# Modulation by selector products, gate weights converted early, and ScalarE's copies of the turned maxima ahead of its exponential

## The chip, the cores and the metric

The kernel runs on one core of a Trainium2 chip. The time is device microseconds of one execution of the whole program. The core has five engines, each with its own queue of instructions in order: TensorE (PE; its weight loads are shown apart as PEld), VectorE (DVE), ScalarE (ACT), GpSimd (POOL) and SyncE (SP, which here issues the transfers between the chip's memory and the core). They meet through semaphores. TensorE writes its sums to PSUM banks, from which VectorE and ScalarE read.

## The reference, cut to what matters

A backbone of two layers over 2,048 latent tokens (a grid of 32 rows of 64) and 256 context tokens, each of width 1,024. Per layer:

```
shift, scale, gate = split(silu(c) @ w_ada + b_ada, 3)      # 3 x 1024; context tokens have their own c
h   = rmsnorm(x) * (1 + scale) + shift
z   = h @ w_in                                              # one projection, cut into 12 column groups
A   = Re(fft2(u)) @ w_four            * silu(gate A)        # 4 Fourier groups of 64
B   = softmax(q k + bias | q kc) [v; vc] * silu(gate B)     # 6 heads of 64, window 8 x 16, plus context keys
C   = norm(gla(q, k, v, decay))       * silu(gate C)        # 4 heads, linear attention in both directions
x   = x + gate * (concat(A, B, C) @ w_out)
```

At the end stands a last RMSNorm. Context tokens pass through the first layer with the same weights and read only context tokens.

## The kernel before

**Order.** The order of nearly all work is written by hand. `Pin` (L64) wraps an engine so that each call keeps the place it has in the program; every instruction recorded that way bears the line of that wrapper, L72, so the profile's groups are told apart by the names of their tiles. PSUM has four names of banks, `a`, `b`, `c`, `pj`, with two buffers each.

**Modulation in the prologue** (L1683 to L1774). The rows of `w_ada` for shift and scale come in eight chunks of 1 MB and 256 columns (`load_r`, L168). `mm_r` multiplies a chunk by the two columns `sil` (the token's and the context's silu(c)): the 8 blocks of the contraction go to 4 groups of TensorE's columns, so the bank holds four partial sums of two rows, on partitions 0, 32, 64 and 96. `fin_r` (L180) copies the first sum with ScalarE, adds the other three with VectorE, and turns the 2x256 row into columns by two transposes into the same bank; VectorE adds the bias (`ada_sc`). `mod` (L189) makes from it the factor `modA` and the summand `modS`, with a common scale for float16. To find the largest value over all partitions it makes a diagonal `dg` with ScalarE, multiplies it by `ones` and reduces the product.

**Weights.** `w_steps` (L468) turns a group of columns of `w_in` into a high and a low float16 part, as a list of small steps: the load, four maxima over quarters (VectorE), empty steps (`lag`), the product with `dg`, the inverse, four high parts (ScalarE) and four low ones (VectorE). `fx` and `fg` are the Fourier group's input and gate.

**Norm and first projections.** Token tiles go in pairs. `norm_a` squares and sums (ScalarE), `norm_b` multiplies (VectorE), `put_a` transposes (TensorE, banks b and c), `put_e` scales by modulation (`hu`) in four groups of two blocks, and writes the high part `hx` (a cast on VectorE) and the low part (a difference on GpSimd, in the last group on VectorE). `four_x` and `four_g` (L320, L327) project. Pair 0 is the context (block 4); the steps of `fg` hang on `put_e`, two after each group:

```
norm_a(1)
norm_b(1)
put_e(s0, 0, [pairs[0], pairs[0] + 1], ra[0], V=v, S=s, G=g, hook=lambda k: step(wg, 2))
```

**Attention** (`na`, from L519). The work is cut into units (p, b): a pair of heads p and a block b of 512 latent tokens (256 context tokens for b = 4); 15 units in layer 0, 12 in layer 1. `fill` (L889) merges the steps of a unit by due times between 0 and 1: packs of scores (TensorE into bank a, VectorE adds the bias table into `pt`), `flush` (the pack's exponential: ScalarE `pt`, its float16 part `ph`, GpSimd the rest `pl`), the products with the values (bank c), the next unit's q and its largest scores, and side jobs. The largest scores of a row (`mh`) are turned by TensorE into bank b and copied into `Q2s` (step `fin`, L729), of which the next unit's scores are made: one copy on ScalarE, one on VectorE. A unit's result is finished in the next one by four steps of `tail` (L757): the last multiplies the gate `gt` by the reciprocal sum, the output `ob` by that, both on GpSimd, and stores `mixd`. Their due times are 0, 1, 2 and 3 parts of a unit.

**Side jobs.** During the attention of layer 0 the modulation of layer 1 is made in steps (`chunk`, L136): load, matmuls, four additions on VectorE onto a row that holds the bias, one empty step, two transposes and a VectorE copy. Chunks 8 to 11 are the gate of the residual and are stored. `wo_scale` (L1481) finds the scale of the output weights, with two empty steps ahead of its product with `dg`.

Of the kernel before, what the change touches and what calls it, by code (L numbers as in the profile page):

```python
# [9 lines left out]
F32 = mybir.dt.float32  # L10
# [67 lines left out]
def body(ctx: ExitStack, tc: tile.TileContext, a, out, dbg=None):  # L78
# [52 lines left out]
    def ada(l, pool):  # L131
        nw = pool.tile([P, KB], F32, tag="ada_nw", name="ada_nw", bufs=1)
        sc = pool.tile([P, 2, 16], F32, tag="ada_sc", name="ada_sc", bufs=1)
        nc.sync.dma_start(out=nw, in_=a["nwcol"][l])

        def chunk(c, pool=pool):  # L136
# [4 lines left out]
            def s0():  # L141
                d["w"] = pool.tile([P, KB * 256], F32, tag="ws", name="ws", bufs=1).rearrange("p (k n) -> p k n", k=KB)
                nc.sync.dma_start(out=d["w"], in_=a["w_ada"][l, c])
                d["row"] = pool.tile([P, 256], F32, tag="row", name="ada_row", bufs=1)[0:2, :]
                nc.sync.dma_start(out=d["row"], in_=a["b_ada"][l:l + 1, c * 256:(c + 1) * 256].to_broadcast([2, 256]))

            def s1():
                pt = d["pt"] = bank("b")
                for k in range(KB):
                    o = k % 4 * 32  # L150
                    te.matmul(out=pt[o:o + 2, 0:256], lhsT=sil[:, k, :], rhs=d["w"][:, k, :], start=(k < 4), stop=(k >= 4))

            def s1b():
                pt = d["pt"]
                for o in range(0, P, 32):
                    v.tensor_tensor(out=d["row"], in0=pt[o:o + 2, 0:256], in1=d["row"], op=ALU.add)
                if c >= 8:
                    nc.sync.dma_start(out=gated[l][:, (c - 8) * 256:(c - 7) * 256], in_=d["row"])

            def s2():  # L160
                pt = bank("b")
                for q in range(2):
                    te.transpose(out=pt[:, 2 * q:2 * q + 2], in_=d["row"][:, q * P:(q + 1) * P], identity=ident[0:2, 0:2])
                v.tensor_copy(sc[:, :, 2 * c:2 * c + 2], pt[:, 0:4].rearrange("p (q w) -> p w q", w=2))
# [8 lines left out]
        def mm_r(w, te):  # L173
            pt = bank("a")
            for k in range(KB):
                o = k % 4 * 32
                te.matmul(out=pt[o:o + 2, 0:256], lhsT=sil[:, k, :], rhs=w[:, k, :], start=(k < 4), stop=(k >= 4))
            return pt

        def fin_r(c, pool, pt, bc, te, v, s):  # L180
            row = pool.tile([2, 256], F32, tag="ada_row2", name="ada_row2", bufs=2)
            s.copy(out=row, in_=pt[0:2, 0:256])
            for o in range(32, P, 32):
                v.tensor_tensor(out=row, in0=pt[o:o + 2, 0:256], in1=row, op=ALU.add)
            for q in range(2):
                te.transpose(out=pt[:, 256 + 2 * q:258 + 2 * q], in_=row[:, q * P:(q + 1) * P], identity=ident[0:2, 0:2])
# [19 lines left out]
        return chunk, mod, (load_r, mm_r, fin_r)  # L206
# [312 lines left out]
    def na(l, last, W, side, st):  # L519
        with ExitStack() as bst:  # L520
# [144 lines left out]
            def st_m(p, b):  # L665
# [63 lines left out]
                def fin():  # L729
# [159 lines left out]
            def fill(i):  # L889
# [48 lines left out]
                sd = side(p, b, wk)  # L938
# [1075 lines left out]
```

## Time and profile before

| | before |
|---|---|
| runs | 2479.67, 2481.02, 2491.21 us |
| median | 2481.02 us |
| profiled execution | 2481.09 us |
| its span | 2479.3 us |
| mean granted clock | 0.979 |
| TensorE, VectorE, ScalarE, GpSimd busy | 2308.9, 1623.3, 1121.3, 1123.5 us |

The span reaches from the first to the last instruction. A row of the timeline gives the start and the length, then the engine, line, operation, the tile written and those read, the shape, and in brackets how long the engine stood before and what ended that. A line of the waits gives the engine and its tile, what it waited for, the total in microseconds, the number of waits and the longest. The shares of the page are means over stages with different limits.

### The profile page before, as it was taken

How to read it: one execution, taken by the hardware profiler on the slowest of the kernel's cores; microseconds unless marked ns; L12 is line 12 of the kernel's file. 1: busy time of each engine (PE TensorE's matmuls, PEld its weight loads, DVE VectorE, ACT ScalarE, POOL GpSimd, SP SyncE). 2: the span in 40 equal slices, each digit the busy share in tenths (PEclk: the TensorE clock that was granted, in tenths of full speed). 3: DMA queues.
4: the chain of work that ended last, by engine and by line, in shares of the span. 5: the costliest groups of instructions: out<-in, count | busy, mean ns of one | idle time of the engine just before them, and what ended most of it. 6: DMA issues, size and time to landing. Idle time of an engine off the chain costs nothing.

```text
span 2479.3 us, 44404 instructions
## 1 busy us (share of the span) xinstructions
PE 2308.9 (93%) x16878; PEld 1540.2 (62%) x16878; DVE 1623.3 (65%) x3625; ACT 1121.3 (45%) x2049; POOL 1123.5 (45%) x1285
## 2 busy tenths in 40 slices
PE   5999998999978999999999999999999799999998
PEld 3555454454546999895444644555555599989443
DVE  5765766676766666696774627667666666679554
ACT  3623554555555444342332225566666534434222
POOL 1524444455544444454553143655555444445343
PEclk7999999999999999999999999999999999999999
DMA  6304124124221110264443021131320211036442
GB/s 256 119 1 137 64 82 114 62 86 125 75 88 59 44 39 31 99 197 160 145 145 119 19 89 32 46 100 52 83 56 24 73 41 38 31 98 208 147 149 98
DMA packets 128622, 225.05 MB, mean 91 GB/s; under 512 B 18724, under 2 KB 81816, under 8 KB 122776
## 3 DMA queue, kind: packets, MB, share of 16 engines
q1 hardware_dynamic: 123224, 212.58, 25.1%
q0 software_dynamic: 5184, 9.64, 2.6%
q8 instruction: 133, 2.18, 0.4%
q14 instruction: 81, 0.66, 0.1%
HBM read 176.79 MB, written 51.37 MB: 92 GB/s over the span
## 4 chain that ended last, share of the span: by engine, by line
PE 36%; DVE 7%; ACT 3%; issue 2%; POOL 1%; DMA 1%; POOLq 0%; SPq 0%; ACTq 0%; DVEq 0%
PE b_pj L72 18%; PE b_a L72 8%; PE b_c L72 4%; PE b_pj L313 3%; PE b_b L72 2%; DVE ot L72 1%; DVE pt L72 1%; ACT pt L72 1%; DVE SU L72 0%; PE b_a L374 0%; DMA rc<-rs 0%; DVE wo L72 0%; DVE w L72 0%; ACT ph L72 0%; DVE gt L72 0%
## 5 line engine op out<-in xcount | busy, mean ns | idle before, releaser
L72 PE MATMUL b_pj<-hx,w 128*128 128x512 f16 (+1 forms) x3168 | 690.0, 364 | 1.8 <-DVE w L72 0.9
L72 POOL TENSOR_TENSOR pl<-pt,ph 128x512 f16<-128x512 f32 (+6 forms) x300 | 306.6, 1024 | 444.2 <-ACT ph L72 368.7
L72 PEld LDWEIGHTS <-w 128*128 128x128 f16 x3168 | 305.6, 99 | 277.1 <-issue 15.8
L72 PEld LDWEIGHTS <-hx 128*128 128x128 f16 x5088 | 435.6, 99 | 5.5
L72 PE MATMUL b_pj<-w,hx 128*128 128x192 f16 (+2 forms) x4272 | 391.4, 250 | 0.0
L72 PE MATMUL b_pj<-wo,m 128*128 128x512 f16 x816 | 302.7, 380 | 0.0
L72 PE MATMUL b_a<-wo,m 128*128 128x512 f16 x816 | 302.4, 380 | 0.0
L72 PEld LDWEIGHTS <-m 128*128 128x128 f16 x1632 | 160.1, 98 | 184.5 <-issue 1.6
L72 DVE SCALAR_TENSOR_TENSOR pt<-b_a,sc,TS 128x160 f32<-128x160 f32 (+4 forms) x432 | 153.0, 400 | 136.9 <-PE b_a L72 99.9
L72 ACT ACTIVATE pt<-pt,psh 128x480 f32<-128x480 f32 (+1 forms) x192 | 121.6, 633 | 169.1 <-DVE pt L72 156.7
L72 PE MATMUL b_c<-ph,vt 128*128 128x320 f16 (+5 forms) x888 | 179.4, 294 | 3.2 <-ACT ph L72 3.2
L72 PEld LDWEIGHTS <-vt 128*128 128x128 f16 x1332 | 120.7, 100 | 94.6 <-issue 31.7
L72 POOL TENSOR_TENSOR xn<-xn,xt 128x512 f32<-128x512 f32 x66 | 110.3, 1692 | 149.0 <-DVE xn L72 117.6
L72 ACT CAST ph<-pt 128x512 f16<-128x512 f32 (+6 forms) x300 | 166.5, 555 | 9.5
L72 PE MATMUL b_c<-pl,vt 128*128 128x320 f16 (+5 forms) x444 | 126.4, 294 | 9.7 <-POOL pl L72 9.6
L72 PE MATMUL b_a<-Q,K 128*128 128x320 f16 (+5 forms) x444 | 120.7, 294 | 13.1 <-ACT Q L72 13.1
L72 DVE CUSTOM_DVE_ANT_0 b_b<-b_b,tmi 128x512 f32<-128x512 f32 (+3 forms) x144 | 86.4, 600 | 69.5 <-PE b_b L72 68.9
L72 PE MATMUL b_a<-q,k 128*128 128x320 f16 (+5 forms) x444 | 121.2, 295 | 4.7 <-DVE MX L72 2.3
L72 ACT ACTIVATE pt<-b_a,psh,sc 128x512 f32<-128x512 f32 (+1 forms) x108 | 81.1, 750 | 78.7 <-PE b_a L72 67.9
L72 PEld LDWEIGHTS <-q 128*128 128x128 f16 x540 | 51.0, 98 | 81.9 <-issue 21.1
L72 POOL TENSOR_TENSOR ats<-ATm 128x512 f32<-128x512 f32 x34 | 43.3, 1272 | 126.9 <-DVE ATm L72 126.9
L313 PE MATMUL b_pj<-hx,w 128*128 128x512 f16 x432 | 96.8, 379 | 0.0
(272 smaller groups left out, 4212.1 us busy)
## 6 DMA issues: line engine op xcount, KB each, us to landing
mx<-mixd SPq DMA_DIRECT2D x34, 512.0 KB
ws<-in_w_in SPq DMA_DIRECT2D x16, 1024.0 KB
xt<-in_x SPq DMA_DIRECT2D x32, 512.0 KB
ws<-in_w_ada SPq DMA_DIRECT2D x16, 1024.0 KB
ws<-in_w_out SPq DMA_DIRECT2D x16, 1024.0 KB
TS<-in_ts SPq DMA_DIRECT2D x12, 1000.0 KB
xres<-xn SPq DMA_DIRECT2D x18, 512.0 KB
qdt_d<-qkT SPq DMA_DIRECT2D x34, 256.0 KB
```

The source lines that it names most:

```text
L72: return self.tc.keep_in_program_order(f(*args, **kw))
L313: te.matmul(out=pt[:, 0:n], lhsT=w[wi][:, k, c0:c0 + P], rhs=r, start=(k == 0 and z == 0), stop=(k == KB - 1 and z == 2))
```

## The change

Six edits.

1. *Selector products.* `silw` holds `sil` in 32 columns, of which 30 are zero, so the four groups fill all 128 partitions. ScalarE copies the whole bank, 128x256, and two products with `sel` (128x2, which sums the partitions 32 apart) replace the additions and the transposes. In the prologue the banks alternate between a and pj. In the attention this holds for chunks 0 to 7, whose bias comes by one transfer `ada_bc` in columns.
2. *Gate weights early.* `fg` is loaded behind the second of the eight chunks, into a place of its own, and its steps run between the chunks.
3. *Pair 1.* Its norm's products move from VectorE to ScalarE, behind the third group of `put_e`; the first projection stands ahead of its transposes.
4. *Turned maxima.* Both copies are on ScalarE, and a `flush` that stood directly ahead of `fin` goes behind it.
5. *Tail.* The last step is due at 4.5 parts in place of 3.
6. *Output weights.* Three empty steps in place of two.

```diff
-        def mm_r(w, te):
-            pt = bank("a")
+        def mm_r(c, w, te, silw):
+            pt = bank(("a", "pj")[c % 2])
             for k in range(KB):
                 o = k % 4 * 32
-                te.matmul(out=pt[o:o + 2, 0:256], lhsT=sil[:, k, :], rhs=w[:, k, :], start=(k < 4), stop=(k >= 4))
+                te.matmul(out=pt[o:o + 32, 0:256], lhsT=silw[:, k, :], rhs=w[:, k, :], start=(k < 4), stop=(k >= 4))
             return pt
 
-        def fin_r(c, pool, pt, bc, te, v, s):
-            row = pool.tile([2, 256], F32, tag="ada_row2", name="ada_row2", bufs=2)
-            s.copy(out=row, in_=pt[0:2, 0:256])
-            for o in range(32, P, 32):
-                v.tensor_tensor(out=row, in0=pt[o:o + 2, 0:256], in1=row, op=ALU.add)
+        def fin_r(c, pool, pt, bc, sel, te, v, s):
+            row = pool.tile([P, 256], F32, tag="ada_row2", name="ada_row2", bufs=2)
+            s.copy(out=row, in_=pt[:, 0:256])
             for q in range(2):
-                te.transpose(out=pt[:, 256 + 2 * q:258 + 2 * q], in_=row[:, q * P:(q + 1) * P], identity=ident[0:2, 0:2])
+                te.matmul(out=pt[:, 256 + 2 * q:258 + 2 * q], lhsT=row[:, q * P:(q + 1) * P], rhs=sel, start=True, stop=True)
...
             def s0():
...
+                if c == 0:
...
+                    lz["bc"] = bcl = lz["wk"].tile([P, 16], F32, tag="ada_bc", name="ada_bc", bufs=1)
+                    with nc.allow_non_contiguous_dma("bias in columns"):
+                        nc.sync.dma_start(out=bcl, in_=a["b_ada"][l, 0:2048].rearrange("(j p) -> p j", p=P))
...
             def s1b():
                 pt = d["pt"]
+                if c < 8:
+                    d["row"] = lz["wk"].tile([P, 256], F32, tag="adar", name="adar", bufs=1)
+                    Pin(tc, S).copy(out=d["row"], in_=pt[:, 0:256])
+                    return
                 for o in range(0, P, 32):
                     v.tensor_tensor(out=d["row"], in0=pt[o:o + 2, 0:256], in1=d["row"], op=ALU.add)
...
                     for h in range(2):
                         o = 64 - h * 64
-                        (v.tensor_copy if h else s.copy)(out=Q2s[h, ev][o:o + 64, 0:n], in_=pmt[o:o + 64, 0:n])
+                        s.copy(out=Q2s[h, ev][o:o + 64, 0:n], in_=pmt[o:o + 64, 0:n])
...
-                    ev += [(min(0.01 + 3.0 * q / T_, 0.09 * q + 0.01), z) for q, z in enumerate(tail(*units[i - 1], ds[i - 1]))]
+                    ev += [(min(0.01 + 3.0 * q / T_, 0.09 * q + 0.01), z) for q, z in zip((0, 1, 2, 4.5), tail(*units[i - 1], ds[i - 1]))]
...
-                return [z for _, z in sorted(ev, key=lambda z: z[0])]
+                ev = [z for _, z in sorted(ev, key=lambda z: z[0])]
+                for z in fs:
+                    k = n = ev.index(z)
+                    while callable(ev[n - 1]) and ev[n - 1] is not flush:
+                        n -= 1
+                    if ev[n - 1] is flush:
+                        ev.insert(k, ev.pop(n - 1))
+                return ev
...
-        return [s0, s1] + ([lambda: None, lambda: None, s1b, s2] if c == 3 else [])
+        return [s0, s1] + ([lambda: None] * 3 + [s1b, s2] if c == 3 else [])
...
-        wg = w_steps(0, "fg", lambda w: W0.__setitem__("g", w), pin=True, tag="pj")
+        wg = w_steps(0, "fg", lambda w: W0.__setitem__("g", w), pin=True, sc=False, tag="pj", lag=2, stage=lambda n: ah.tile([P, n], F32, name="ws2", bufs=1))
...
-        ws = [load_r(c, ah) for c in range(4)]
+        ws = [load_r(c, ah) for c in range(2)]
+        step(wg)
+        ws += [load_r(c, ah) for c in range(2, 4)]
...
             step(wx, 2)
+            if c > 1:
+                step(wg, 3)
         fetch(1)
-        step(wg)
         fetch(2)
         step(wx, 99)
...
+        step(wg, 99)
...
         norm_a(1)
-        norm_b(1)
-        put_e(s0, 0, [pairs[0], pairs[0] + 1], ra[0], V=v, S=s, G=g, hook=lambda k: step(wg, 2))
+
+        def norm_1(k):
+            if k == 3:
+                for q in range(2):
+                    s.activation(out=xs[1][:, q, :], in_=xs[1][:, q, :], func=AF.Copy, scale=rs[1][q])
+
+        put_e(s0, 0, [pairs[0], pairs[0] + 1], ra[0], V=v, S=s, G=g, hook=norm_1)
+        Wg["scales"]()
         fetch(3)
         for n, (f, b) in enumerate(((0, 4), (1, 4), (0, 3), (1, 3), (0, 2), (1, 2), (0, 1), (1, 1), (0, 0)), 1):
-            if n < len(pairs):
-                put_a(n)
-                put_b(n)
+            def put(n=n):
+                if n < len(pairs):
+                    put_a(n)
+                    put_b(n)
+
+            if n > 1:
+                put()
...
                 four_x(ug[0], b, Wx, te=te, s=s)
+            if n == 1:
+                put()
```

The prologue on TensorE, from the modulation's end to the first projection, before: `ident,ada_row` is the turning of the last chunk, `dg,ones` the two scales (of the modulation and of `fg`), `ident,xt` the transposes of pair 1.

```order
L72 MATMUL b_a_300<-ident_69,ada_row2_327 128x2 x2
L72 MATMUL b_pj_353<-dg_351,ones_71 128x128
L72 MATMUL b_pj_397<-dg_390,ones_71 128x128
L72 MATMUL b_b_412<-ident_69,xt_318 128x128 x4
L72 MATMUL b_c_417<-ident_69,xt_318 128x128 x4
L72 MATMUL b_b_422<-ident_69,xt_318 128x128 x4
L72 MATMUL b_c_427<-ident_69,xt_318 128x128 x4
L72 LDWEIGHTS w2_241
L72 MATMUL b_pj_477<-hx_83,w2_241 128x256
```

The same place after (`sel,ada_row` is the selector product of the last chunk):

```order
L72 MATMUL b_pj_310<-ada_w_224,silw_111 32x256 x8
L72 MATMUL b_a_291<-sel_114,ada_row2_319 128x2 x2
L72 MATMUL b_pj_310<-sel_114,ada_row2_332 128x2 x2
L72 MATMUL b_pj_355<-dg_353,ones_71 128x128
L72 LDWEIGHTS w2_243
L72 MATMUL b_pj_404<-hx_83,w2_243 128x256
```

The scale of `fg` and the four groups of transposes no longer stand between the modulation's scale and the first projection; the transposes follow its last matmul.

ScalarE in the second unit of layer 1, before: `pt` and `ph` are the exponentials of two packs, `w` a part of a weight conversion, `Q` the copy of the turned maxima, `gt` the gate.

```order
L72 ACTIVATE pt<-pt,psh 128x320
L72 CAST ph<-pt 128x320
L72 ACTIVATE pt<-pt,psh 128x440
L72 CAST ph<-pt 128x440
L72 ACTIVATE w_16675<-ws,wsm 128x512
L72 CAST Q_01_16012<-b_b 64x512
L72 ACTIVATE gt<-b_pj,wsm 128x512
```

And after:

```order
L72 ACTIVATE pt<-pt,psh 128x320
L72 CAST ph<-pt 128x320
L72 ACTIVATE w_16631<-ws,wsm 128x512
L72 CAST Q_01_15968<-b_b 64x512
L72 CAST Q_11_15982<-b_b 64x512
L72 ACTIVATE pt<-pt,psh 128x440
L72 CAST ph<-pt 128x440
L72 ACTIVATE gt<-b_pj,wsm 128x512
```

The second pack's exponential has moved behind both copies, of which there was one here.

GpSimd in unit (0, 3) of layer 1, before: `q` are the low parts of the next unit's q, `K` those of keys, `gt` and `ob` the tail's last step.

```order
L72 TENSOR_TENSOR pl<-pt,ph 128x480
L72 TENSOR_TENSOR gt<-gt,rs 128x512
L72 TENSOR_TENSOR ob<-ob,gt 128x512
L72 TENSOR_TENSOR q_17397<-qf,q_17397 64x512
L72 TENSOR_TENSOR q_17401<-qf,q_17401 64x512
L72 TENSOR_TENSOR pl<-pt,ph 128x400
L72 TENSOR_TENSOR K_05_16015<-kf,k_17458 64x256
L72 TENSOR_TENSOR K_15_16029<-kf,k_17462 64x256
```

And after:

```order
L72 TENSOR_TENSOR q_17350<-qf,q_17350 64x512
L72 TENSOR_TENSOR q_17354<-qf,q_17354 64x512
L72 TENSOR_TENSOR pl<-pt,ph 128x400
L72 TENSOR_TENSOR K_05_15971<-kf,k_17411 64x256
L72 TENSOR_TENSOR K_15_15985<-kf,k_17415 64x256
L72 TENSOR_TENSOR gt<-gt,rs 128x512
L72 TENSOR_TENSOR ob<-ob,gt 128x512
```

The two products of the tail have gone behind q, one pack's rest and two keys.

## Rows read from the trace of the kernel before

**Rows 1.** Page, the span and each engine's busy time

```profile
span 2479.3 us, 44404 instructions
PE 2308.9 (93%) x16878; PEld 1540.2 (62%) x16878; DVE 1623.3 (65%) x3625; ACT 1121.3 (45%) x2049; POOL 1123.5 (45%) x1285
```

**Rows 2.** Waits of TensorE, whole program; us in total, times, longest

```profile
PE b_a L72 <- ACT Q L72: 13.1, 15, 2.1
PE b_b L72 <- ACT dg L72: 12.6, 9, 3.6
...
PE b_b L72 <- DVE mh L72: 11.0, 16, 1.6
...
PE b_pj L72 <- ACT dg L72: 9.8, 2, 8.0
...
PE b_b L72 <- DVE ada_row L72: 9.4, 7, 2.1
PE b_b L72 <- POOL q L72: 9.2, 9, 2.6
```

**Rows 3.** Timeline of the prologue, 33 to 72 us; start us, us, instruction

```profile
33.80 1.89 PE L72 MATMUL b_a<-ada_w,sil 128*2 128x256 f32 x16 [0.25 <-DVE ada_sc L72]
...
37.13 1.33 DVE L72 TENSOR_TENSOR ada_row<-b_a,ada_row 2x256 f32<-2x256 f32 x3
...
38.98 0.16 DVE L72 TENSOR_TENSOR ada_sc<-b_a,bc 128x4 f32<-128x4 f32 x1 [0.52 <-PE b_a L72]
...
42.80 0.55 ACT L72 ACTIVATE hu<-b_b,modS,modA 128x256 f32<-128x256 f32 x1
...
49.51 0.80 PE L72 MATMUL b_pj<-dg,ones 128*128 128x128 f32 x2 [8.04 <-ACT dg L72]
...
53.51 6.47 PE L72 MATMUL b_pj<-hx,w 128*128 128x256 f16 x48
...
71.79 0.38 PE L72 MATMUL b_pj<-hx,w 128*128 128x512 f16 x1
```

**Rows 4.** Windows; PE, PEld, DVE, ACT, POOL busy, PEclk, DMA share, GB/s

```profile
25.00:30.00 5.00, 3.59 (x34) 0.98 (x26) 3.23 (x10) 2.47 (x5) 0.00 (x0) 0.50 1.00 410
30.00:35.00 5.00, 4.04 (x36) 1.37 (x36) 3.79 (x10) 1.35 (x3) 0.00 (x0) 0.50 0.42 160
```

**Rows 5.** Timeline, VectorE and GpSimd at the first `hx`, 44 to 47 us

```profile
44.40 0.75 DVE L72 TENSOR_SCALAR xt<-xt,rst 128x1024 f32<-128x1024 f32 x1 [0.72 <-POOL rst L72]
...
46.21 1.15 POOL L72 TENSOR_TENSOR hx<-hu,hx 128x512 f16<-128x512 f32 x1 [1.85 <-DVE hx L72]
```

**Rows 6.** Timeline around a Q copy in layer 1, 1533 to 1539 us

```profile
1533.48 0.52 PE L72 MATMUL b_b<-idb,mh 128*32 128x128 f16 x16
...
1535.71 0.66 ACT L72 ACTIVATE pt<-pt,psh 128x440 f32<-128x440 f32 x1 [3.70 <-DVE pt L72]
...
1537.04 1.02 POOL L72 TENSOR_TENSOR pl<-pt,ph 128x440 f16<-128x440 f32 x1 [4.17 <-ACT ph L72]
...
1537.61 0.58 ACT L72 CAST Q<-b_b 64x512 f16<-64x512 f32 x1
...
1538.24 0.38 PE L72 MATMUL b_a<-Q,K 128*128 128x512 f16 x1 [2.06 <-ACT Q L72]
```

**Rows 7.** Tile Q: ns min/median/max, starts, forms; and who waited

```profile
L72 ACT CAST Q<-b_b x27: 367/581/582, 243.5 to 1923.4; 64x512 f16<-64x512 f32 x24, 64x256 f16<-64x256 f32 x3
L72 DVE CAST Q<-b_b x27: 415/683/684, 244.1 to 1924.0; 64x512 f16<-64x512 f32 x24, 64x256 f16<-64x256 f32 x3
...
  DVE Q L72: 43.4, 25
```

**Rows 8.** Timeline, TensorE in unit (0, 3) of layer 1

```profile
1592.42 0.31 PE L72 MATMUL b_b<-k,q 128*128 128x320 f16 x1 [2.61 <-POOL q L72]
```

**Rows 9.** Waits of SyncE's queue, small transfers in the attention

```profile
SPq L768 <- DMA rc<-rs: 31.3, 26, 2.5
```

**Rows 10.** Timeline, TensorE at the output weights' scale

```profile
722.75 0.79 PE L72 MATMUL b_b<-dg,ones 128*128 128x128 f32 x2 [3.60 <-ACT dg L72]
```

More of the change, by code (lines that the diff above doesn't have):

```diff
@@ L143, in s0 @@
                 nc.sync.dma_start(out=d["w"], in_=a["w_ada"][l, c])
-                d["row"] = pool.tile([P, 256], F32, tag="row", name="ada_row", bufs=1)[0:2, :]
-                nc.sync.dma_start(out=d["row"], in_=a["b_ada"][l:l + 1, c * 256:(c + 1) * 256].to_broadcast([2, 256]))
+                if c == 0:
+                    lz["silw"] = z = pool.tile([P, 256], F32, tag="row", name="silw1", bufs=1).rearrange("p (k m) -> p k m", k=KB)
+                    v.memset(z, 0.0)
+                    v.tensor_copy(z[:, :, 0:2], sil)
+                    lz["bc"] = bcl = lz["wk"].tile([P, 16], F32, tag="ada_bc", name="ada_bc", bufs=1)
+                    with nc.allow_non_contiguous_dma("bias in columns"):
+                        nc.sync.dma_start(out=bcl, in_=a["b_ada"][l, 0:2048].rearrange("(j p) -> p j", p=P))
+                    lz["sel"] = z = lz["wk"].tile([P, 2], F32, tag="ada_sel", name="sel1", bufs=1)
+                    v.tensor_reduce(out=z, in_=ident.rearrange("p (g c) -> p c g", c=32)[:, 0:2, :], op=ALU.add, axis=AX.X)
+                if c >= 8:
+                    d["row"] = pool.tile([P, 256], F32, tag="row", name="ada_row", bufs=1)[0:2, :]
+                    nc.sync.dma_start(out=d["row"], in_=a["b_ada"][l:l + 1, c * 256:(c + 1) * 256].to_broadcast([2, 256]))
             def s1():
@@ L162, in s2 @@
                 for q in range(2):
-                    te.transpose(out=pt[:, 2 * q:2 * q + 2], in_=d["row"][:, q * P:(q + 1) * P], identity=ident[0:2, 0:2])
-                v.tensor_copy(sc[:, :, 2 * c:2 * c + 2], pt[:, 0:4].rearrange("p (q w) -> p w q", w=2))
+                    te.matmul(out=pt[:, 2 * q:2 * q + 2], lhsT=d["row"][:, q * P:(q + 1) * P], rhs=lz["sel"], start=True, stop=True)
+                v.tensor_tensor(out=sc[:, :, 2 * c:2 * c + 2], in0=pt[:, 0:4].rearrange("p (q w) -> p w q", w=2), in1=lz["bc"][:, 2 * c:2 * c + 2].unsqueeze(1).to_broadcast([P, 2, 2]), op=ALU.add)
             return [s0, s1, s1b] + ([lambda: None, s2] if c < 8 else [])
@@ L204, in mod @@
             V.tensor_scalar_mul(modS[l], sc[:, :, 0:8], mx[:, 2:3])
-        return chunk, mod, (load_r, mm_r, fin_r)
+        return chunk, mod, (load_r, mm_r, fin_r, lz)
     def rms(pool, xt, junk, S=S, G=G):
@@ L1692, in body @@
         V.tensor_scalar_mul(sil, sil, 0.5)
+        silw = s0.tile([P, KB, 32], F32, name="silw", bufs=1)
+        V.memset(silw, 0.0)
+        V.tensor_copy(silw[:, :, 0:2], sil)
+        sel = s0.tile([P, 2], F32, name="sel", bufs=1)
+        V.tensor_reduce(out=sel, in_=ident.rearrange("p (g c) -> p c g", c=32)[:, 0:2, :], op=ALU.add, axis=AX.X)
         bc = s0.tile([P, 16], F32, name="bc", bufs=1)
@@ L1732, in hook @@
                     norm_b(i + 1)
-                step(wg, 2)
             norm_a(i + 1)
@@ L1799, in body @@
         if not last:
-            chunk, mod, _ = ada(1, wp)
+            chunk, mod, (_, _, _, lz) = ada(1, wp)
             jobs += [chunk(c) for c in range(8)] + [[lambda: mod(Pin(tc, V), Pin(tc, S), Pin(tc, G), Pin(tc, TE))]]
@@ L1805, in body, with side @@
         pre = {}
-        def side(p, b, wk):
+        def side(p, b, wk, bk):
             n = p + 1
             res = []
+            if not last:
+                lz["wk"] = bk
             if b == 0:
```

21 lines of the change are left out of this document (12 added, 9 removed).

## The prediction

> **What bounds the kernel now.** The page comes first: TensorE is busy 2308.9 of 2479.3 us, 93 %, and no other engine is over 65 % [rows 1]. So the sum is made of the stretches in which TensorE stands, and work taken off another engine counts only where TensorE waits for it. The profiled execution took 2481.09 us, 1.8 more than its span and within 0.1 of the median of the runs (2481.02), so a gain read from its trace can be taken off either.
>
> The second view is TensorE's waits by what ended them [rows 2]. Six lines bear on the change: 13.1 us for ScalarE's copies Q of the turned maxima, 12.6 and 9.8 for the diagonals `dg` by which a group of weights gets its scale, 11.0 for VectorE's `mh`, 9.4 for VectorE's `ada_row` (the modulation sums in the attention), 9.2 for GpSimd's q. Together they are 65 us, 2.6 % of the span, which is about all that an edit of these waits could return. The third view is the timeline of the prologue, where single long waits show; the fourth, of the places where the Q, q and `dg` waits are longest.
>
> **The change: prologue.** Two places here.
>
> Step A, the end of the modulation. Before, the eight chunks are chained by VectorE: three additions on two partitions take 1.33 us a chunk, and the next chunk's matmuls of 1.89 us are released by VectorE's `ada_sc`; the last `ada_sc` stands at 38.98 and the first scaled tile `hu` at 42.80 [rows 3]. The change takes out 8 x 1.33 = 10.6 us of VectorE and lets two banks alternate, so the chain breaks. What is late next is the load: the stream runs at 410 GB/s with a DMA share of 1.00 until 30 us, and in the next 5 us moves 160 GB/s x 5 = 0.8 MB, so it ends at 30 + 0.8/0.41 = 32.0 [rows 4]. The gate weights' 1 MB now stand ahead of the third chunk and push the eighth by 1/0.41 = 2.5 us, to where the stream ended before, 32.0. Behind it: matmuls 1.89, a copy of 128x256 at most 0.55 (by the `hu` row), its two sums and the addition, some 0.9; about 35.5 to 36.5, against 38.98. A gain of 2.7 is the upper bound. The lower one is nothing: the weights' eight conversions and four maxima now stand in the same queues of ScalarE and VectorE ahead of the copies. I take 1.5 between them, `hu` at 41.3.
>
> Step B, the first projection. From `hu` at 42.80 it takes until 53.51, 10.7 us. In them TensorE stood 8.04 for the gate weights' `dg`, and behind that the transposes of pair 1 [rows 3]. The change takes both from there: the weights are converted by then, and the transposes follow the first projection. What is late next is `hx`: its first low half ends at 46.21 + 1.15 = 47.36, after VectorE's two products for the norm of pair 1, the second alone 0.75 behind a stall of 0.72 [rows 5]. These products go to ScalarE, to the end of the same step, where the projection's 6.47 us cover them; if that cover is gone they cost, by the columns of the `hu` row, at most 4 x 0.55 each. Without them I estimate 2.9 from `hu` to the projection (bounds 2.4 and 4.6, the latter the present 47.36 - 42.80). That gives back 10.7 - 2.9 = 7.8. Three things take some of it again. The transposes of pair 1 now fall between the first and second projection; they lay in the 3.2 us from 49.51 + 0.80 to 53.51, and I take 2.0. The next pair's norm queues behind the first projection's evacuation; I take 1.7 of new wait (0 to 4). And TensorE's granted clock stood at 0.50 (1.2 GHz) in both stretches of [rows 4]; the first projection now starts 9 us nearer to them and may run at that level for longer: 1.5 (0 to 6.5, all of it at half speed). Left are 7.8 - 5.2 = 2.6, and with step A the third projection starts at 67.7 in place of 71.79: 4.1 us (0 to 9). Behind it the row of projections is bound by TensorE, so the gain stays.
>
> **The change: attention, 27 units.** Five edits.
>
> The Q copies. At 1534 to 1538 one reads the mechanism: TensorE's transposes end at 1534.0. ScalarE, idle 3.70, takes the next score's exponential at 1535.71 first, and copies Q only at 1537.61; TensorE stands 2.06 for it [rows 6]. After the change the copy stands ahead of the exponential and would be done by 1534.7. But the value product behind it needs `pl`, whose GpSimd product ends at 1537.04 + 1.02 = 1538.06, later still by what the copies put off; the scores come forward, the values do not. So I don't count all 13.1 us: 9 (0 to 13.1), as most of the 15 waits have other work queued behind them. The second copy moves from VectorE (0.68 a piece) to ScalarE (0.58): 27 x 0.581 = 15.7 us more on ScalarE, 45 % busy, and 27 x 0.683 = 18.4 less on VectorE, which also stood 43.4 us at its copies, 25 times, in order, with its other work behind [rows 7]. Of what that unblocks (11.0 us of `mh` waits at most) I count 2.
>
> The Trainium skill, "ScalarE: Activation LUTs", section "Rules for kernel authors", speaks against this edit: simple elementwise work belongs on VectorE, up to about 3 times as fast per element in bf16. By it the moved copy would take 3 x 0.683 = 2.05 us, an estimate, and both copies of a unit 2.63; were all of that on the path, 27 x 2.63 = 71 us, the time would be 2481.1 - 15.1 + 71 = 2537 (15.1 being the sum without the Q gain). The trace disagrees for this form, 64x512 from a PSUM bank in float32: 0.581 on ScalarE, 0.683 on VectorE.
>
> The tail's last step. GpSimd's products `gt` and `ob` stand ahead of both q products in a unit of layer 1, and TensorE waits 2.61 for q [rows 8]; the same order recurs once. After the change they stand behind. That is 5 of the 9.2 us (0 to 9.2). What is behind them now is only the store of `mixd` and the next unit's `ob` tile, for which I take 1.5 off.
>
> The modulation sums of chunks 0 to 7: four additions on VectorE become one ScalarE copy of 128x256 (at most 0.55, eight times 4.4 us in all) and a selector product on TensorE in place of the transposes. Of the 9.4 us of waits for VectorE I take 5 (0 to 9.4), as the copy can land behind an exponential of 0.66. Its bias comes by one transfer of single elements, which no row shows. From below it costs nothing; from above I take a whole wait of SyncE for a small transfer, 2.5 us the longest of 26, mean 1.2 [rows 9]. It lies at the start of layer 0 among other loads and I count 0.5.
>
> The Trainium skill, "DMA: Bandwidth & Descriptors", section "Rules for kernel authors", has such a transfer, with its last dimension strided, fall apart into one descriptor per element, here 2,048. With the 10.5 ns per packet of its section "Bandwidth" that is 2048 x 10.5 / 16 = 1.3 us, an estimate; the sum would be 0.8 longer by it. No run so far shows it.
>
> The output weights' `dg`: TensorE waits 3.60 at 722.75 [rows 10]. One more empty step puts its product later, and I take 3.
>
> Against these: ScalarE's added 15.7 + 4.4 us, and exponentials that start up to two copies later, where I take 2 (0 to 31, below). Sum for the attention: 9 + 2 + 5 - 1.5 + 5 - 0.5 + 3 - 2 = 20. With the prologue 24.1, and 2481.1 - 24.1 = 2457.0; I forecast **2457**.
>
> **The rivals.** *Half is given back* (2469): a wait taken from one engine returns at the next. For it: the lines of [rows 2] share their places, since VectorE's `mh`, ScalarE's Q and GpSimd's `pl` follow each other within a unit, and a chain of the three is not shortened by moving one. In the prologue the change may not do what it says, since copies queue behind conversions. Against it: the prologue's 8.04 and the 2.61 are single waits with a clear cause. Half of 24.1 is 12.
>
> *VectorE's relief is large* (2442): the 18.4 us of copies and part of the 43.4 of standing come back on TensorE. For it: 11.0 us of `mh` and other lines with VectorE. Against: VectorE is at 65 % and off the path. Up to 15 us more than forecast.
>
> *Slower: the copies hold up the exponential.* In each of 27 units both copies, 2 x 0.58 = 1.16 us, plus any wait for the transposes, now stand ahead of a pack's exponential; its `pl` product is late by as much, and the value product with it. Were all of it on the path, the Q gain is lost (24.1 - 9 = 15.1 left) and 27 x 1.16 = 31.3 are added: 2481.1 - 15.1 + 31.3 = 2497. It decides from 15.1 / 27 = 0.56 us per unit on. For it: `pl` at 1538.06 is already within 0.2 us of the scores' start. Against it: ScalarE idled 3.70 just there, so a copy mostly fills idle time.
>
> **How the numbers follow.** About 0.5 %, 12.4 us, can be told from no change, so faster means below 2468.6, slower above 2493.4. The forecast has 0.60 (own range 2447 to 2466), half given back 0.25 (2463 to 2477, 0.10 of it faster), relief 0.09, the slower rival 0.06, of which 0.05 lies above 2493.4. Faster 0.60 + 0.10 + 0.09 = 0.79, same 0.15 + 0.01 = 0.16, slower 0.05. The range 2440 to 2474 leaves out the end of the second case (0.05), the slower rival (0.06) and the end of the relief (0.04).
>
> **What would show it.** In the profile after: the first projection at 44 to 45 and the third at 66 to 69; no wait of several us for a `dg` in the prologue; the line of Q from 13.1 to 4 or less, q to 4, `ada_row` replaced by a line of ScalarE of at most 5; ScalarE's busy time up by 15 to 25 and VectorE's down by 30 or more. It is wrong if TensorE's waits for `pl` and `ph`, or for the new copy, grow by more than 5, or if the third projection starts after 71.

## The result, and the profile after

The changed kernel took 2468.05 us (median of 5 runs, 2462.11 to 2471.91) against 2488.99 for the kernel before (5 runs, 2479.67 to 2491.56): a ratio of the means of 0.9925, with a 95 % interval from 0.9897 to 0.9953, some 19 us faster. The runs of the kernel before fall near 2480 us or near 2490, two and three of them here, so that its mean says more than its median. The forecast was 2457 with a range from 2440 to 2474; the sign was right. By the median the size is nearer to the second case, half given back, at 2469; by the ratio, taken off the 2481.1 that the forecast started from, it is 2462.5 and lies between the two.

The page after, span and busy time:

```profile
span 2465.9 us, 44388 instructions
PE 2319.8 (94%) x16910; PEld 1550.2 (63%) x16910; DVE 1592.3 (65%) x3546; ACT 1135.7 (46%) x2086; POOL 1119.2 (45%) x1285
```

Against [rows 1] the span is 13.4 us shorter, and the two halves of that are worth seeing apart. TensorE stands 2465.9 - 2319.8 = 146.1 us in place of 170.4, 24.3 us less, as much as the whole sum was. But it is busy 10.9 us more, of which the sum had 1.5. Of these, 6.9 lie in the first 75 us (50.6 against 43.7 us busy); the other 4 come in an execution with a mean granted clock of 0.974, against 0.979 for the kernel before. VectorE lost 31 us and ScalarE gained 14.

TensorE's waits after (what it waited for, total, times, longest):

```profile
PE b_c L72 <- POOL pl L72: 8.6, 16, 0.9
PE b_a L72 <- DMA k<-k: 7.1, 11, 1.0
PE b_c L72 <- ACT ph L72: 5.9, 5, 2.9
...
PE b_b L72 <- POOL q L72: 4.2, 7, 1.1
...
PE b_b L72 <- DVE ada_row L72: 1.2, 1, 1.2
...
PE b_a L72 <- ACT Q L72: 0.5, 2, 0.4
```

Beside [rows 2]: Q fell from 13.1 to 0.5, q from 9.2 to 4.2, `ada_row` from 9.4 to 1.2. New is a line that before did not have: 7.1 us, 11 times, for swapped keys `k`, and longer waits for `w_ada` (3.0 to 5.2) and for `ph` (3.2 to 5.9).

The prologue after, TensorE (start, us, instruction, idle before):

```profile
20.21 1.94 PE L72 MATMUL b_a<-ada_w,silw 128*32 128x256 f32 x16 [3.06 <-DMA ada_w<-in_w_ada]
22.08 1.02 PE L72 MATMUL b_pj<-sel,ada_row 128*128 128x2 f32 x4
...
36.26 1.94 PE L72 MATMUL b_pj<-ada_w,silw 128*32 128x256 f32 x16
...
47.45 7.94 PE L72 MATMUL b_pj<-hx,w 128*128 128x256 f16 x47 [0.94 <-POOL hx L72]
55.23 0.60 PE L72 MATMUL b_b<-ident,xt 128*128 128x128 f32 x4
...
60.41 0.45 PE L72 MATMUL b_b<-ident,xt 128*128 128x128 f32 x1 [3.28 <-DVE xt L72]
61.88 0.90 PE L72 MATMUL b_b<-ident,xt 128*128 128x128 f32 x3 [1.02 <-DVE xt L72]
...
64.29 1.06 PE L72 MATMUL b_c<-ident,xt 128*128 128x128 f32 x4
...
72.81 2.54 PE L72 MATMUL b_pj<-hx,w 128*128 128x512 f16 x11
```

The window of the modulation (busy of TensorE, its weight loads, VectorE, ScalarE and GpSimd, granted clock, DMA share, GB/s):

```profile
20.00:40.00 20.00, 19.20 (x128) 10.88 (x128) 9.07 (x25) 7.32 (x15) 0.00 (x0) 0.50 0.99 403
```

And ScalarE's first scaled tiles of pairs 0 and 1:

```profile
44.47 0.55 ACT L72 ACTIVATE hu<-b_b,modS,modA 128x256 f32<-128x256 f32 x1
...
58.02 0.55 ACT L72 ACTIVATE hu<-b_b,modS,modA 128x256 f32<-128x256 f32 x1
```

In [rows 3] `hu` came at 42.80, the first projection at 53.51, the third at 71.79. Now they come at 44.47, 47.45 (but for one matmul) and 72.81: the first projection is 6 us earlier and the third 1 us later. Pair 1's scaling waits until 58.02, because its transposes stand behind the first projection. For the third projection one trace is not enough: five runs below have the same prologue, and there it starts between 71.18 and 73.57.

The place of [rows 6] after, TensorE, ScalarE and GpSimd at a Q copy in layer 1:

```profile
1533.33 0.52 PE L72 MATMUL b_b<-idb,mh 128*32 128x128 f16 x16
...
1533.92 1.18 ACT L72 CAST Q<-b_b 64x512 f16<-64x512 f32 x2 [1.44 <-PE b_b L72]
...
1535.56 0.66 ACT L72 ACTIVATE pt<-pt,psh 128x440 f32<-128x440 f32 x1 [0.45 <-DVE pt L72]
...
1536.88 1.02 POOL L72 TENSOR_TENSOR pl<-pt,ph 128x440 f16<-128x440 f32 x1 [4.16 <-ACT ph L72]
```

Both copies now fill ScalarE's idle time, and the exponential behind them still waits 0.45 for VectorE's sum, so the copies delay nothing here. From the transposes to `pl` there are 3.55 us, before 3.56.

The end of layer 0's attention after, ScalarE and TensorE, with ScalarE's line of waits:

```profile
ACT ob L72 <- DMA mixd<-ob: 31.9, 12, 4.8
```

```profile
709.12 0.68 ACT L72 ACTIVATE ob<-b_c,gsc 64x512 f32<-64x512 f32 x1 [3.21 <-DMA mixd<-ob]
...
712.18 0.43 PE L72 MATMUL b_c<-ph,vt 128*128 128x160 f16 x2 [2.93 <-ACT ph L72]
```

ScalarE stands 3.21 us for the store of the unit before, since `ob` has one tile; the next exponential stands behind it, and TensorE 2.93 us behind that. Before, this line was 1.6 us, once.

### The profile page after: what moved, and what is told of

Same layout as the page of the kernel before. It is cut to its first block, busy times and chain, and to the rows that moved or that the text cites. A ratio compares the mean times of both kernels' runs of the same rounds, so it can differ in the third digit from the quotient of the medians.

```text
span 2465.9 us, 44388 instructions
## 1 busy us (share of the span) xinstructions
PE 2319.8 (94%) x16910; PEld 1550.2 (63%) x16910; DVE 1592.3 (65%) x3546; ACT 1135.7 (46%) x2086; POOL 1119.2 (45%) x1285
## 2 busy tenths in 40 slices
DMA packets 130653, 225.04 MB, mean 91 GB/s; under 512 B 20772, under 2 KB 83848, under 8 KB 124808
```

## The experiments

Ratios are to the kernel before, with their 95 % interval. "Kernel after" is the changed one, 0.9925.

**The prologue alone.** The kernel before with edits 1 (in the prologue), 2 and 3; the diff is against the kernel after and cut to two of its places, the second to the end of a line.

```diff
-                        s.copy(out=Q2s[h, ev][o:o + 64, 0:n], in_=pmt[o:o + 64, 0:n])
+                        (v.tensor_copy if h else s.copy)(out=Q2s[h, ev][o:o + 64, 0:n], in_=pmt[o:o + 64, 0:n])
...
-zip((0, 1, 2, 4.5), tail(*units[i - 1], ds[i - 1]))
+enumerate(tail(*units[i - 1], ds[i - 1]))
```

> The kernel before with the prologue's part of the change alone (selector products there, early gate weights, pair 1's norm on ScalarE, first projection ahead of pair 1's transposes); the attention is that of before. Theory (the prologue gave nothing: its weights and selector products made TensorE and the load the bound): third projection at 72 to 74 us against 71.79 before, first Q copy of the attention at 244 to 245.5 against 243.50, and the whole time within 0.3 % of before (ratio 0.997 to 1.003). Rival (the prologue does gain, and something in the attention hides it): first Q copy before 242 and a ratio under 0.997.

Measured 0.9989 (0.9978 to 1.0000). The third projection stood at 71.18, the first Q copy 0.4 us earlier than before: a little earlier than expected, but the prologue returns 0 to 5 us, not more. Even that is in doubt: in the other five traces with this order of the prologue (the kernel after and four runs below) the third projection starts at 71.84 to 73.57 and the first Q copy 0.3 to 2.0 us later than before. TensorE is busy 2322.2 us in this kernel against 2308.9. Of the 13.3 more, 6.3 lie in the first 75 us (49.9 against 43.7), so these are the prologue's; the others lie in an attention that is that of before, in an execution with a mean granted clock of 0.973 against 0.979.

**The attention alone.** The kernel before with edits 1 (for layer 1), 4, 5 and 6; against the kernel after, the prologue's edits are taken back, of which two places are shown.

```diff
-        ws = [load_r(c, ah) for c in range(2)]
-        step(wg)
-        ws += [load_r(c, ah) for c in range(2, 4)]
+        ws = [load_r(c, ah) for c in range(4)]
...
-            if n > 1:
-                put()
+            if n < len(pairs):
+                put_a(n)
+                put_b(n)
```

> The kernel before with the attention's part of the change alone (selector products for layer 1's modulation, both Q copies on ScalarE ahead of the exponential, the tail's last step at 4.5, three empty steps); the prologue is that of before. Theory: third projection at 71.8 and first Q copy at 243.5 as before; all of the gain is here, so the time is that of the changed kernel or 1 us less, ratio 0.990 to 0.994. Rival (prologue and attention share it): a ratio of 0.995 or more.

Measured 0.9913 (0.9899 to 0.9927). All of the gain that can be told from noise lies here.

**The tail at 3 parts.** The end of the one changed line:

```diff
-zip((0, 1, 2, 4.5), tail(*units[i - 1], ds[i - 1]))
+enumerate(tail(*units[i - 1], ds[i - 1]))
```

> The changed kernel with the tail's last step due at 3 parts again in place of 4.5. Theory (the later step holds the one tile of ob longer): ScalarE's waits for the store of ob fall from 31.9 us (12 times) to about 2, and the 2.93 us that TensorE stands for an exponential at 712 us, behind such a wait, goes; against it TensorE's wait for q rises from 4.2 to about 9. The time is within 3 us of the changed kernel, faster by 3 to 4 in layer 0 and slower by 3 to 5 in layer 1. Rival (the later step is worth the 5 us that were forecast and costs nothing): 5 us slower than the changed kernel. Second rival (ScalarE's waits cost TensorE in every unit): 6 us or more faster.

Measured 0.9893 (0.9874 to 0.9912), 0.0032 or some 8 us under the kernel after: the second rival. The two intervals overlap a little, but the next run, taken with this one and with its tail at 4.5, has 0.9926 (0.9913 to 0.9939). ScalarE's line:

```profile
ACT ob L72 <- DMA mixd<-ob: 1.8, 2, 1.0
```

TensorE's wait for q came back as expected (9.5 us), and is worth 5 us; the later step cost more than that. The line for swapped keys is gone, and so is the long wait for `w_ada`. The store is not what held that load up: in the kernel after SyncE issues the store at 526.42, and the load 12.5 us later, when VectorE's `wsm` releases it.

```profile
526.42 0.35 SPq L793 DMA_DIRECT2D mixd<-ob  x1
...
538.90 9.24 SPq L144 DMA_DIRECT2D ws<-in_w_ada  x2
```

The load then took longer to land (SyncE's next step stood 6.6 us for it, 4.6 here); why is open. There the clock shows too. This kernel, and then the kernel after, at the same chunk:

```profile
540.16 1.05 PE L72 MATMUL b_b<-ws,sil 128*2 128x256 f32 x16 [1.24 <-DMA ws<-in_w_ada]
541.14 1.47 PE L72 MATMUL b_pj<-hx,w 128*128 128x512 f16 x6
```

```profile
545.85 1.89 PE L72 MATMUL b_b<-ws,sil 128*2 128x256 f32 x16 [3.74 <-DMA ws<-in_w_ada]
547.67 2.74 PE L72 MATMUL b_pj<-hx,w 128*128 128x512 f16 x6
```

The stretch of 20 us around them, this kernel and the kernel after (columns as in the window above):

```profile
530.00:550.00 20.00, 18.76 (x128) 9.78 (x127) 9.44 (x25) 9.30 (x19) 5.39 (x8) 1.00 0.33 107
```

```profile
540.00:560.00 20.00, 16.26 (x103) 7.18 (x104) 4.32 (x10) 6.37 (x13) 3.63 (x5) 0.83 0.30 105
```

Behind a stand of 3.74 us the same 22 matmuls take 4.6 us in place of 2.5, at 1.2 GHz by their length and by the clock of the stretch, 0.83; behind a stand of 1.24 us the clock stayed at 1.00. So 2.5 us more of waiting cost 4.6. The next run shows it a second time (1.89 and 2.74 us behind a stand of 2.91). Not every kernel with the later tail lost the clock there: the attention alone, which stood 2.76, has 1.04 and 1.47.

**Pair 2 behind the second projection too.**

```diff
-            if n > 1:
+            if n > 2:
                 put()
...
-            if n == 1:
+            if n <= 2:
                 put()
```

> The changed kernel with pair 2's transposes and scaling behind the second projection too, so that the norm of pair 2 has a projection beside it. Theory (the change took the cover from that norm): the waits of 3.28 and 1.02 us for VectorE's xt at 60 to 62 us go, the granted clock stays up there, the third projection starts at 66 to 68 in place of 72.81, the first Q copy at 239 to 240.5, and the time is 4 to 6 us under the changed kernel. Rival (the norm is late whatever stands ahead): a wait of 2 us or more for xt stays, ahead of the third projection, which starts at 71 or later.

Measured 0.9926 (0.9913 to 0.9939): the same time as the kernel after. The wait moved one step on, and the third projection started at 72.02, as the rival had it:

```profile
67.33 0.45 PE L72 MATMUL b_b<-ident,xt 128*128 128x128 f32 x1 [4.20 <-DVE xt L72]
```

So the cover was not what was missing. A new theory: the pairs follow each other through ScalarE, VectorE and GpSimd, and what counts is when pair 1 begins.

**Pair 1's transposes first again.**

```diff
-            if n > 1:
-                put()
+            put()
...
-            if n == 1:
-                put()
```

> The changed kernel with pair 1's transposes and scaling ahead of the first projection again, as before; the weights and the modulation stay as changed. Theory (the pairs are paced by ScalarE's, VectorE's and GpSimd's work on them, some 7.5 us a pair, and the change let pair 1 start it 8 us later): pair 1's first scaled tile at 50 to 52 us in place of 58.0, no wait over 1.5 us for xt ahead of the second projection, third projection at 68 to 71 in place of 72.8. Rival (the first projection's early start is worth what was forecast, and only the weights' place in the load delays it all): the third projection at 75 or later, and the time 2 to 4 us over the changed kernel.

Measured 0.9917 (0.9897 to 0.9936).

```profile
49.26 0.47 PE L72 MATMUL b_b<-ident,xt 128*128 128x128 f32 x1 [6.40 <-ACT xt L72]
...
67.71 10.52 PE L72 MATMUL b_pj<-hx,w 128*128 128x512 f16 x48
```

```profile
52.37 0.55 ACT L72 ACTIVATE hu<-b_b,modS,modA 128x256 f32<-128x256 f32 x1
```

TensorE stands 6.40 us here for pair 1, whose first scaled tile is 0.4 us later than expected, and the third projection still comes 5.1 us earlier than in the kernel after, 0.3 before the range expected; in time the two cannot be told apart by their intervals, in the trace they can. But the start of pair 1 is not all: the kernel before scaled its first tile of pair 1 at 49.37, earlier than either, and had the third projection at 71.79. There TensorE stood 0.92 us in the second projection for the gate weights' low part `w` and 1.13 ahead of it for a scaled tile, and it made the first projection in 6.47 us, here in 5.58.

**The products at 3, the store at 4.5.**

```diff
-                    nc.sync.dma_start(out=mixd[l][b][:, 2 + p, :], in_=ob)
-                return [in_, rec, bc_, fin]
+                def sto():
+                    nc.sync.dma_start(out=mixd[l][b][:, 2 + p, :], in_=d["ob"][:, 0:n])
+                return [in_, rec, bc_, fin, sto]
...
-zip((0, 1, 2, 4.5), tail(*units[i - 1], ds[i - 1]))
+zip((0, 1, 2, 3, 4.5), tail(*units[i - 1], ds[i - 1]))
```

> The changed kernel with the tail's two products at 3 parts again and only its store at 4.5: SyncE's queue no longer stands for the product, but the one tile of ob is still given back late. Theory (the standing queue was the cost): TensorE's 7.1 us of waits for swapped keys go, ScalarE's waits for the store of ob stay at 15 us or more, and the time is that with the tail at 3, ratio to before 0.987 to 0.991. Rival (the held tile was the cost): a ratio of 0.992 or more.

Measured 0.9893 (0.9875 to 0.9911), as with the tail at 3. But ScalarE's waits for `ob` were 3.8 us and not 15: the late store did not hold the tile, so this run separates nothing.

**The store from GpSimd's queue.**

```diff
-                    nc.sync.dma_start(out=mixd[l][b][:, 2 + p, :], in_=ob)
+                    g.dma_start(out=mixd[l][b][:, 2 + p, :], in_=ob)
```

> The changed kernel with the store of ob issued from GpSimd's queue in place of SyncE's, the products still at 4.5. Theory (the standing queue was the cost): no wait of TensorE for swapped keys, the wait of 3.7 us for w_ada at 546 us back to 1 to 1.6, wait for q still at 4, so a ratio of 0.986 to 0.990, the best so far, if GpSimd's own issue costs nothing. Rival (the held tile was the cost): ScalarE's waits stay near 30 us and the ratio is 0.992 or more.

Measured 0.9926 (0.9910 to 0.9942): the rival. The line for swapped keys is gone, `w_ada` is down to 2.6 us, q stays at 4.2, and nothing came of it, while ScalarE's line grew:

```profile
ACT ob L72 <- DMA mixd<-ob: 53.5, 19, 6.3
```

GpSimd is busy 20 us more in it (1139.6), so the free queue and the longer held tile are mixed.

**The Q copies alone.** The kernel before with edit 4.

```diff
-                        (v.tensor_copy if h else s.copy)(out=Q2s[h, ev][o:o + 64, 0:n], in_=pmt[o:o + 64, 0:n])
+                        s.copy(out=Q2s[h, ev][o:o + 64, 0:n], in_=pmt[o:o + 64, 0:n])
...
+                for z in fs:
+                    k = n = ev.index(z)
+                    while callable(ev[n - 1]) and ev[n - 1] is not flush:
+                        n -= 1
+                    if ev[n - 1] is flush:
+                        ev.insert(k, ev.pop(n - 1))
```

> The kernel before with one part alone: both Q copies on ScalarE, and a flush that stood directly ahead of them behind them. Theory: TensorE's wait for Q goes from 13.1 to under 2 us; VectorE is freed of 18 us, and the time falls by 8 to 12 us (ratio 0.995 to 0.997), little of it given back at ph and pl. Rival (the copies hold up the exponential and the wait returns there): TensorE's waits for ph and pl, 3.2 and 9.6 before, rise by 5 or more together and the ratio is 0.998 or more. Second rival (VectorE's relief is large): a ratio under 0.994.

Measured 0.9929 (0.9914 to 0.9944), the second rival: by itself this edit is worth nearly what all six are, 17.6 us. Its lines:

```profile
PE b_c L72 <- POOL pl L72: 10.9, 16, 2.5
...
PE b_c L72 <- ACT ph L72: 2.7, 4, 1.1
```

TensorE's wait for Q is down to 1.6 us. `ph` and `pl` are 13.6 us together, 12.8 before: next to nothing returns there. And `ada_row` falls from 9.4 to 4.1 with the four additions still on VectorE. The wait for the output weights' `dg` falls too, from 3.60 to 2.73, though its empty steps are two as before.

**The last product into the gate's tile.** The tail stays at 4.5.

```diff
-                    g.tensor_tensor(out=ob, in0=ob, in1=gt, op=ALU.mult)
-                    nc.sync.dma_start(out=mixd[l][b][:, 2 + p, :], in_=ob)
+                    g.tensor_tensor(out=gt, in0=ob, in1=gt, op=ALU.mult)
+                    nc.sync.dma_start(out=mixd[l][b][:, 2 + p, :], in_=gt)
```

> The changed kernel, tail still at 4.5, with the tail's last product written into the gate's tile and stored from there, so that the one tile of ob comes free with the product and not with its store. SyncE's queue stands for the product as in the changed kernel. Theory (ScalarE stands at the held tile, and the exponentials behind it): ScalarE's waits for ob fall from 31.9 us to under 12, TensorE's wait of 2.9 for ph at the end of layer 0's attention goes, and the ratio to before is 0.988 to 0.991. Rival (the queue behind the store was the cost): waits for swapped keys stay at 7 us and the ratio stays at 0.992 to 0.994.

Measured 0.9904 (0.9882 to 0.9926), median 2460.54. The first fence is ScalarE's waits, the second SyncE's, the third TensorE's:

```profile
ACT ob L72 <- POOL gt L72: 8.5, 5, 2.7
...
ACT ob L72 <- POOL K L72: 4.4, 5, 0.9
```

```profile
SPq L793 <- POOL gt L72: 210.1, 26, 13.7
```

```profile
PE b_a L72 <- DMA k<-k: 7.0, 11, 1.0
...
PE b_c L72 <- ACT ph L72: 3.0, 3, 1.3
```

SyncE's queue stands 210 us as in the kernel after (210.3; 153.5 before), the keys are as late, and by the ratios two thirds of the tail's cost are gone with ScalarE's waits (12.9 us left, a little over the 12 expected). The interval overlaps those of the tail at 3 and of the kernel after, so the share is rough.

**Both edits taken back.** The kernel after with the tail at 3 and pair 1 first (the two diffs above).

> The changed kernel with two of its edits taken back: the tail's last step at 3 parts, and pair 1's transposes ahead of the first projection. Theory (both cost time and add up): third projection at 67 to 69, first Q copy at 239 to 241, ScalarE's waits for ob under 4 us, ratio to before 0.985 to 0.989. Rival (what one gives back the other loses): a ratio of 0.989 or more.

Measured 0.9878 (0.9856 to 0.9900), median 2454.31, third projection at 68.43: the fastest in this study together with the next.

**The gate weights behind the chunks.** The run above, with:

```diff
-        ws = [load_r(c, ah) for c in range(2)]
-        step(wg)
-        ws += [load_r(c, ah) for c in range(2, 4)]
+        ws = [load_r(c, ah) for c in range(4)]
...
-            if c > 1:
+            if c == 3:
+                step(wg)
+            if c > 5:
                 step(wg, 3)
...
         def norm_1(k):
+            step(wg, 2)
```

> The kernel of the run before this one with the gate weights loaded behind all eight chunks and converted beside the scaling of pair 0. Theory (the weights' place in the load delayed the modulation by the 3 us that TensorE stands at the third chunk): that wait goes, the first scaled tile at 41 to 42.5 us in place of 44, the third projection 1 to 3 us earlier. Rival (TensorE's own products, 1.94 and 1.02 us a chunk at half clock, bound the modulation, and the conversions cost more beside the scaling): first scaled tile at 43 or later, or a third projection no earlier.

Measured 0.9879 (0.9857 to 0.9900), no difference. The first scaled tile at 43.78 and the third projection at 69.50: the rival.

```profile
17.65 1.07 PE L72 MATMUL b_a<-ada_w,silw 128*32 128x256 f32 x16 [0.30 <-DMA ada_w<-in_w_ada]
...
37.90 1.01 PE L72 MATMUL b_pj<-sel,ada_row 128*128 128x2 f32 x4 [2.84 <-ACT ada_row L72]
```

The wait at the third chunk is gone, and the time is lost again along the chunks and at the last copy: moving the weights gains nothing. Whether that wait cost anything by itself stays open, since the conversions moved with the load.

**Both copies on ScalarE, the order as before.** The first line of the diff of the Q copies, without the loop.

> The kernel before with both Q copies on ScalarE, and the order of the exponential as before, ahead of them. Theory (the order makes the gain: a copy that stands behind an exponential waits for VectorE's sum): TensorE's wait for Q stays at 10 us or more and the ratio is 0.996 to 1.000. Rival (VectorE's relief makes it): a ratio of 0.992 to 0.995 with the wait for Q still there.

Measured 0.9966 (0.9952 to 0.9980), about 8 us, with TensorE's wait for Q untouched:

```profile
PE b_a L72 <- ACT Q L72: 13.1, 15, 2.1
...
PE b_b L72 <- DVE ada_row L72: 4.1, 4, 1.4
```

What the relief does shows at the first chunk of the modulation. In the kernel before VectorE stands 1.98 us at its Q copy, its additions come behind that, and TensorE waits for them:

```profile
283.24 0.68 DVE L72 CAST Q<-b_b 64x512 f16<-64x512 f32 x1 [1.98 <-ACT Q L72]
283.84 1.76 DVE L72 TENSOR_TENSOR ada_row<-b_b,ada_row 2x256 f32<-2x256 f32 x4
...
285.75 0.25 PE L72 MATMUL b_b<-ident,ada_row 2*128 2x2 f32 x2 [2.12 <-DVE ada_row L72]
```

With both copies on ScalarE the additions start 2.8 us earlier and nobody waits:

```profile
281.01 1.77 DVE L72 TENSOR_TENSOR ada_row<-b_b,ada_row 2x256 f32<-2x256 f32 x4 [0.40 <-PE b_b L72]
...
283.27 0.28 PE L72 MATMUL b_b<-ident,ada_row 2*128 2x2 f32 x2
```

Theory and rival each hold in part: the order is worth the 9 us between 0.9966 and 0.9929, VectorE's relief the other 8. Of these 8 the trace shows some 5: TensorE stands 165.6 us, 170.4 before.

## Why the prediction was right, and where it was not

The sum was 24.1 us, the measured change 18.6 (12 to 26 by the interval of the ratio). Of the signs that the prediction named, those of the attention came: Q at 0.5, q at 4.2, VectorE down by 31.0, `pl` and `ph` together up by only 1.7 (ScalarE's 14.4 more is just under the 15). Those of the prologue did not: the first projection came at 47.45 for 44 to 45, and the third at 72.81, behind the 71 that the prediction itself had called a sign of being wrong. Its terms fared so:

*The Q copies.* The order was put at 9 us and measured at 9. VectorE's relief was put at 2 and measured at 8 (5 to 12): this is the term that was mis-sized. It was looked for in the line of `mh`, which did not move (11.0, 11.0 with the copies on ScalarE), and it came at `ada_row`, 9.4 to 4.1, and at the output weights' `dg`, 3.60 to 2.73: VectorE's 43.4 us of standing at Q [rows 7] had stood ahead of its other work, at 283.24 us ahead of the modulation's additions. The cost of 2 at the exponential did not appear: `pl` and `ph` rose by 0.8, and at [rows 6] ScalarE had idled 3.70 us. The rule of the Trainium skill ("ScalarE: Activation LUTs", "Rules for kernel authors") that simple elementwise work belongs on VectorE, with its factor for bf16, does not hold for this form, a float32 bank copied to float16, by the copies' prices [rows 7] and by this time.

*The tail.* Put at 5 us of gain less 1.5; measured as a loss of 8 (0.9925 against 0.9893). The gain at q was right, 9.2 to 4.2. What failed is the sentence on what is late next: "only the store of `mixd` and the next unit's `ob` tile", 1.5. The tile was held so long that ScalarE stood 31.9 us for it, with exponentials behind it, and SyncE's queue 57 us more, with keys behind. Writing the product into another tile took ScalarE's waits away and returned some two thirds of the loss, so the held tile is shown to be a cause, its size roughly; whether the queue is the rest stays open, since the run that freed it lengthened the hold. TensorE's waits are not all of it: with the new prologue and the tail's products at 4.5 it stands 145.6 to 147.5 us in four traces (the kernel after, both runs that move transposes, the store from GpSimd), with the products at 3 it stands 141.1 to 143.9 in four, which is some 3.5 us of the 8. The rest shows as busy time, which varies with the granted clock from one execution to the next, so where it was lost stays open. Two buffers for `ob` were not tried.

*Step A.* Put at 1.5 us earlier, measured 1.7 later. The sum looked at the load's end and at VectorE, and missed that each pair of selector products takes 1.02 us of TensorE at half clock where the two transposes of the kernel before had taken 0.34:

```profile
33.20 0.34 PE L72 MATMUL b_a<-ident,ada_row 2*128 2x2 f32 x2 [0.22 <-DVE ada_row L72]
```

Chunks that follow without a wait are 2.81 us apart after (33.45 and 36.26), with TensorE busy throughout, and were 2.71 apart before (31.09 and 33.80). VectorE's chain was replaced by TensorE's, which is no shorter, and the third chunk began 2.3 us later than before (20.21 against 17.92), behind the wait of 3.06 for its load. Loading the gate weights behind all chunks did not bring the first scaled tile forward, as said. The bound of 2.7 was also too low by its own terms: 38.98 less 35.5 to 36.5 is 2.5 to 3.5.

*Step B.* The estimate of 2.9 us from `hu` to the projection was right (2.98), and so was 1.5 for the clock (7.94 against 6.47), the latter by luck: with the first projection as before, four traces have 5.40 to 6.47 for it. The new wait was put at 1.7 and was 4.3 (3.28 and 1.02), and the transposes behind it ran at the granted clock's lower level (0.50 from 62 to 65 us; 1.06 us for four, 0.60 ahead of the stand at a clock of 1.00). The step that failed is that the first projection's start was worth its gain: what bounds these 25 us in the changed kernel is when pair 1 starts through the scaling, as the run with its transposes first shows, 5.1 us earlier at the third projection. The prologue as a whole gave 0 to 5 us where 4.1 were forecast.

*Modulation and output weights.* Put at 5 - 0.5 + 3 = 7.5. By ratios, 0.9893 / (0.9929 x 0.9989) = 0.9975 leaves 6 us for both, with an uncertainty as large; no run had them alone. In the traces only half of that shows. The selector products took `ada_row` from 4.1 to 1.2, the rest of its fall being the relief's. The wait for the output weights' `dg` went from 3.60 to 2.59, but it is 2.73 with the Q copies alone and two empty steps, and 2.73 with the tail at 3 and three of them: the third empty step, counted at 3 us, bought 0.1 or nothing, and this term failed whole. The bias transfer came as 2,048 packets under 512 B more (20,772 against 18,724), one per element as the Trainium skill has it ("DMA: Bandwidth & Descriptors", "Rules for kernel authors"). No engine waited for it: it was issued at 218.8 us and first read at 285.8. So the 0.5 counted for it was not paid, and no row shows the 1.3 us, whose division by 16 is the prediction's own step and not the Trainium skill's.

So the total was near by luck, because two errors of opposite sign met: 8 us too little for the Q copies (6 of relief, and the 2 of cost that did not come) and 11 too much for the tail; the prologue and the rest were 1 or 2 too high each by their middle values. Each of these differences has an uncertainty of several us, and they add up only if the edits do not touch each other. Taking back the two edits that cost gives 0.9878.

## What to carry to other kernels

A copy that stands ahead of its consumer on two engines, one behind the other, costs the second engine's standing too: look up who that engine serves next before putting its relief low. When a step is moved later, price the buffer that it holds, by the number of buffers, and look at the in-order queue in which its transfer waits, not only at what it stood in the way of. When a wait shrinks behind several edits, look at the run that has only one of them before giving it to the edit that was meant for it. Starting the first user early gains nothing if the producers of the second start later for it.

## What the runs showed of the chip that was not expected

Two products of a 128x128 float32 tile with two columns took 1.02 us on TensorE at the half clock, three times the two transposes that they replaced, though they move only two columns. And a stand of 3.74 us cost more than itself: 22 matmuls behind it took 4.6 us at 1.2 GHz, 2.5 behind a stand of 1.24.
